# One-core transformer stack on Trainium2: paired decay matmuls, a finer weaving of side chains, and a two-pass layer norm

## The chip, the cores and the metric

The kernel runs on one core of a Trainium2 chip. The metric is the device time of one execution in microseconds. Five engines work side by side and wait for each other by semaphores: TensorE (PE in the profile, its weight loads PEld), VectorE (DVE), ScalarE (ACT), GpSimd (POOL) and SyncE (SP), which here issues the weight transfers. TensorE's clock has two levels, 1.2 and 2.4 GHz; the profile gives the level as the granted clock, 0.50 and 1.00.

## The reference, cut to what matters

One batch of 256 tokens of width 1024 goes through four layers. The first two begin with a mixer of four branches that all read the same projection of the input, and end with a feed-forward part (dense in layer 0, eight experts with two per token in layer 1). The last two are a different block (gated attention, linear attention, cross attention, feed-forward) that the change doesn't touch.

```
y = mixer_block(x, ...)                       # swa, rwkv7, fox, dsa; each gated and projected, then summed
x = layer_norm(4**0.25 * x + y, ln_g, ln_b)   # (x - mu) * rsqrt(var + 1e-5) * g + b
y = swiglu(x) or moe_ffn(x)
x = layer_norm(4**0.25 * x + y, ln_g, ln_b)
```

The branches: swa is window attention with sinks (8 heads), rwkv7 a linear recurrence with a state for each of 4 heads, fox causal attention whose logits get a decay term (the cumulative sum of log-sigmoid gates, query's minus key's, 4 heads), dsa attention over the keys that an index score picks (the 64 best for this mask). All is in float32 to within the kernel's splits.

## The kernel before, in words

**Tiling.** 256 tokens are two tiles of 128 (t = 0, 1). A large product runs on values split in two: each weight chunk that arrives from memory (a `raw` or `af` tile, 128x1024) is copied by ACT to a rounded high part `wh` (line 550) and DVE subtracts to get the low part `wl` (line 552); activations are split the same way (`split`, line 493; `transpose_split`, line 647, transposes four 128x128 blocks on PE and then splits them into `ar` tiles). Three matmuls (high by high, low by high, high by low) then accumulate. The group `mm<-wh,ar` is this work. Everything small (softmax, recurrence, index scores) is in plain float32, which the trace shows as two matmul records for each matmul.

**Weaving in the mixer.** From line 844 on, the mixer lists its weight blocks in a fixed order (`plan`). Inside this part PE's order and the weight transfers on SP are the program's (lines 391, 546). The four branches are Python generators, called chains, that yield at points where PE would have to wait for DVE or ACT. The kernel keeps a counter `vt` of planned PE time (`pe`, line 388; a 128x512 matmul of a chunk counts 512/2.4+13 ns). `yield 6.0` means: not before `vt` has grown by 6.0. After each weight chunk `pump` (line 435) looks whether `vt` grew by `PUMP` since its last turn; if so, each chain that is due issues its next step. A chunk is six 128x512 matmuls, about 1.36 in the counter, or six 128x256 ones, about 0.72. `finish` (line 443) issues what is left of a chain at once, when the main stream needs its result.

**The chains.** `dsa` (line 1022): index scores by PE, then on DVE eight rounds of the eight largest and a replacement, the mask `mk` (line 1053), then `attend`, whose first matmuls add the mask to the logits by an identity matmul (line 809). `fox` (line 982): the cumulative gates give `A` and `B2`; each head's logits are one matmul with 8 rows (line 1014) and one with 64 rows (line 1015). `swa` (line 970) has 64-row logits only. `attend` (line 801) works on two banks of two heads; for heads 0 to 3 it alternates the lower and upper 64 partitions, each half writing to a bank of its own. `_rwkv_tile` (line 1091), once for each token tile: projections, an inverse square root on DVE (line 1147) and a transpose of its result (line 1150), a blocked triangular inverse (lines 1241 to 1265), two chunks of the recurrence (lines 1273 to 1320), a group norm, and the gated result `ofs[t]`. The mixer waits for both rwkv chains at line 947 and transposes their results there (line 948), before branch 1.

**Softmax scaling.** `softmax_pair` (line 764) scales each head's probabilities by the reciprocal sum: in the mixer on ACT (line 785), elsewhere on DVE (line 787).

**Layer norm.** `ln_apply` (line 1382) runs four times: after the mixer and after the feed-forward part of layers 0 and 1, the last without a transpose. For each token tile and each half of 512 columns it makes three passes on DVE (lines 1396 to 1398) and then one `transpose_split` (line 1400).

Of the kernel before, what the change touches and what calls it, by code (L numbers as in the profile page):

```python
# [193 lines left out]
RP = 0  # L194
AHEAD = 0
LOOK = 4
PUMP = 2.0
FIT = 16
AR_SMALL = 512
SMALL = 4  # L200
# [64 lines left out]
class Net:  # L265
# [498 lines left out]
    def softmax_pair(self, lg, nk, scale, sink=None):  # L764

        nm = self.T([128, 2], "nm")
        sm = self.T([128, 2], "sm")
        self.nc.vector.tensor_reduce(nm, lg, axis=AX.X, op=OP.max)  # L768
        if sink is None:
            self.ts(nm, nm, -scale, OP.mult)  # L770
        else:
            self.stt(nm, nm, scale, sink, OP.mult, OP.max)
            self.ts(nm, nm, -1.0, OP.mult)
        P = self.T([128, 2, nk], "P")
        for g in range(2):
            self.act(P[:, g, :nk], lg[:, g, :], AF.Exp, scale=scale, bias=nm[:, g:g + 1], accum_out=sm[:, g:g + 1])
        if sink is not None:
            es = self.T([128, 2], "es")
            self.add(es, sink, nm)
            self.act(es, es, AF.Exp)  # L780
            self.add(sm, sm, es)
        self.nc.vector.reciprocal(sm, sm)
        for g in range(2):
            if self.woven:
                self.act(P[:, g, :nk], P[:, g, :nk], AF.Copy, scale=sm[:, g:g + 1])
            else:
                self.ts(P[:, g, :nk], P[:, g, :nk], sm[:, g:g + 1], OP.mult)
        return P
# [9 lines left out]
        self.act(PT[:, :2 * kt], p)  # L798
        return PT

    def attend(self, t, nk, scale, banks, qk, v, O, f, sinks=(None, None), mask=None, tag="ps"):

        with self.scope():
            kt = nk // 128
            lgs = [self.ps([128, 2, nk]) for _ in banks]
            st = True
            if mask is not None:
                for lg in lgs:
                    self.mmul(lg, self.identb, mask[:, None, :].to_broadcast([128, 2, nk]), True, False)
                st = False  # L810
            for j in range(2):
                for b in range(2):
                    qk(lgs[b][:, j, :], banks[b][j], t, nk, st)
            Ps = [self.softmax_pair(lgs[b], nk, scale, sinks[b]) for b in range(2)]
            yield 6.0
            PTs = []
            for P in Ps:
                PTs.append(self.pT(P, nk, tag))
                self.free(P)
            yield 3.0  # L820
            o = self.bank(tag, [128, 2, 128])
            for j in range(2):
                for k in range(kt):
                    for b in range(2):
                        self.mmul(o[b * 64:(b + 1) * 64, j], v(banks[b][j], k), PTs[b][:, j * kt + k], k == 0, k == kt - 1)
            sl = (slice(None), slice(f, f + 2), slice(t * 128, (t + 1) * 128))
            self.split(O[0][sl], O[1][sl], o)
            yield 1.0


    def mixer(self, l, X, x, st):
# [4 lines left out]
        with self.scope():  # L836
# [55 lines left out]
            O1 = newO(2)  # L892

            rk = self.rwkv(l)
            ofs = {}
            recs = [self.spawn(self.rwkv_tile(l, t, prs, rk, ofs)) for t in range(2)]
            for f, ps in self.lin_fm(X, w, 3):
                self.act(kv[:, 0, :], ps[:, 0])
# [46 lines left out]
            gates(0)  # L945
            for t in range(2):
                self.finish(recs[t])
                self.transpose_split(O1, t, ofs[t])
                self.free(ofs[t])
            branch(1, O1)  # L950
            self.finish(at0)
            self.free(q2)
# [29 lines left out]
    def fox(self, qk_, tv, O):  # L982
        nc = self.nc

        lf = self.T([128, 2, 16], "lf")
        nc.vector.memset(lf, 0.0)
        xx = self.T([128, 2, 4], "fx")
        self.add(xx, tv[:, :, 448:452], self.rrs[:, None, 0:4].to_broadcast([128, 2, 4]))
        e = self.T([128, 2, 4], "fe")
        self.stt(e, xx, -1.0, xx, OP.mult, OP.max)  # L990
        self.act(e, e, AF.Exp, scale=-1.0)
        self.act(e, e, AF.Ln, bias=1.0)
        self.stt(lf[:, :, 0:4], xx, 0.0, e, OP.min, OP.subtract)
        self.ts(lf[:, :, 12:16], lf[:, :, 0:4], -1.0, OP.mult)
        yield 3.0

        p = self.ps([8, 2, 256])
        for g in range(2):
            self.mmul(p[:, g, :], lf[:, 0, g * 8:g * 8 + 8], self.cum0, True, False)
            self.mmul(p[:, g, 128:256], lf[:, 1, g * 8:g * 8 + 8], self.le, False, False)  # L1000
            self.mmul(p[:, g, :], self.sel8[0:1, g, :], self.ones[0:1, :], False, True)
        A = self.T([8, 4, 256], "fA")
        B = self.T([8, 256], "fB")
        for h in range(4):
            self.ts(A[:, h, :], p[:, 0, :], self.hsel[:, h:h + 1], OP.mult)
        self.act(B, p[:, 1, :])
        B2 = self.T([8, 256], "fB2")

        self.ts(B2, B, 8.0, OP.mult)
        yield 3.0  # L1010

        def qk(out, h, t, nk, st):
            sl = slice((h % 2) * 64, (h % 2) * 64 + 64)
            self.mmul(out, A[:, h, t * 128:(t + 1) * 128], B2[:, 0:nk], st, False)
            self.mmul(out, qk_[sl, h // 2, t * 128:(t + 1) * 128], qk_[sl, 2 + h // 2, 0:nk], False, True)

        yield from self.pipeline([
            self.attend(t, 128 * (t + 1), 0.125, ((0, 2), (1, 3)), qk,
                        lambda h, k: tv[:, k, 128 + h * 64:192 + h * 64], O, 0, mask=(self.mc0, self.mc1)[t])
            for t in range(2)])  # L1020

    def dsa(self, q, kd, ki, qi, tv, O):
        nc = self.nc
        REP = -3e38
        for t in range(2):
          with self.scope():
            nk = 128 * (t + 1)
            ww = self.T([128, 4], "ww")
            self.ts(ww, tv[:, t, 452:456], 0.5, OP.mult)
            sc = self.T([128, 256], "sc")  # L1030
            rls = [self.T([128, 2, 256]) for _ in range(2)]
            pk = [self.ps([128, 2, nk]) for _ in range(2)]
            for i in range(2):
                for g in range(2):
                    sl = slice(g * 64, g * 64 + 64)
                    self.mmul(pk[g][:, i], qi[sl, i, t * 128:(t + 1) * 128], ki[sl, 0:nk], True, True)
            for g in range(2):
                self.act(rls[g][:, :, :nk], pk[g], AF.Relu, scale=0.125)
            yield 1.0
            for i in range(2):  # L1040
                for g in range(2):
                    h = 2 * i + g
                    self.stt(sc[:, :nk], rls[g][:, i, :nk], ww[:, h:h + 1], self.ad[:, 256 - nk:] if h == 0 else sc[:, :nk],
                             OP.mult, OP.add)
            self.free(*rls)
            m8 = self.T([128, 8], "m8")
            for r in range(8):
                nc.vector.max(out=m8, in_=sc[:, :nk])
                nc.vector.match_replace(out=sc[:, :nk], in_to_replace=m8, in_values=sc[:, :nk], imm_value=REP)
                if r % 2:  # L1050
                    yield 1.5
            mk = self.T([128, 256], "mk", BF)
            self.ts(mk[:, :nk], sc[:, :nk], -2e38, OP.is_gt, -1e30, OP.mult)

            self.free(sc)

            def qk(out, h, t, nk, st):
                sl = slice((h % 2) * 64, (h % 2) * 64 + 64)
                self.mmul(out, q[sl, h // 2, t * 128:(t + 1) * 128], kd[sl, 0:nk], st, True)

            yield from self.attend(t, nk, 0.125, ((0, 2), (1, 3)), qk, lambda h, k: tv[:, k, 384:448], O, 0, mask=mk[:, :nk])
# [29 lines left out]
    def _rwkv_tile(self, l, t, prs, end, rc, hw, Sts, wa, gu, ofs):  # L1091
# [53 lines left out]
            self.mmul(p[:, 2 * i:2 * i + 2], sq[:, i], self.ind2, True, True)  # L1145
        rs = T([128, 4])
        self.rsqrt(rs, p, [128, 4], 1.0, 1e-12)
        yield 4.0
        p = self.pr([4, 128])
        self.tr(p, rs, self.ident)  # L1150
        rsT = T([4, 128])
# [175 lines left out]
        self.mul(vv, vt.rearrange("p (h s) -> p h s", h=4), bo[:, :, None].to_broadcast([128, 4, 64]))  # L1327
        self.add(o, o, vv)
        self.mul(of, o.rearrange("p h s -> p (h s)"), gm)
        yield 10.0  # L1330

    def groupnorm(self, pY, g, b):
        sm = self.T([128, 4], "gsm")
# [48 lines left out]
    def ln_apply(self, x, l, i, st, X=None):  # L1382

        nc = self.nc
        with self.scope():
# [4 lines left out]
            for t in range(2):  # L1390
                nc.vector.bn_aggr(out=mv[t], in_=st[t])
                self.rsqrt(rs[t], mv[t][:, 1:2], [128, 1], 1.0, 1e-5)
                for b in range(2):
                    sl = slice(b * 512, (b + 1) * 512)
                    v = x[t][:, sl]
                    self.ts(v, v, mv[t][:, 0:1], OP.subtract, rs[t], OP.mult)
                    self.mul(v, v, g[:, sl])
                    self.add(v, v, be[:, sl])
                    if X is not None:
                        last = self.transpose_split(X, t, v, k0=4 * b)  # L1400
                if X is not None and t == HOLD_T:
                    self.hold = (last, 2)
        self.free(*st)
# [731 lines left out]
```

## Time and profile before

| what | value |
|---|---|
| median of 3 runs | 2149.79 us (2149.65 to 2153.29) |
| the profiled execution's own time | 2148.88 us |
| its span, first to last instruction | 2147.2 us |
| PE busy | 2079.5 us (97%) |
| DVE busy | 1495.5 us (70%) |
| ACT busy | 1163.1 us (54%) |
| mean granted clock | 0.981 |
| moved by DMA | 411.37 MB, mean 192 GB/s |

The span is 1.68 us shorter than that execution's time, and that execution 0.91 us below the median. Busy time of PE counts overlapping matmuls once, and a matmul at the lower clock counts as busy as one at the higher. In a timeline row the first two numbers are the start and the length of a run of like instructions; the square bracket at its end is the idle time of the engine just before it and what ended it.

### The profile page before, as it was taken

Reading aid. Unit: us, or ns where it says so; the run is one execution under the profiler, and the core shown is the slowest. Engines: PE = TensorE matmul, PEld = TensorE weight load, DVE = VectorE, ACT = ScalarE, POOL = GpSimd, SP = SyncE. Lnnn points to the kernel's source line nnn. Section 1 sums busy time; section 2 is a strip of 40 time slices with the busy share of each in tenths; the row PEclk is TensorE's granted clock in tenths of the full one; section 3 lists DMA queues with packets and bytes.
Section 4 is the critical chain, followed back from the end, with each engine's and each line's share of the span. In section 5 each row is a group of like instructions: output and inputs, shape, how many; then the busy total and the mean of one; then the engine's idle time right before and its main releaser. Section 6 shows DMA issues by size and latency. Waiting matters only on the chain. (4 is left out here: it accounts for less than half of the span.)

```text
span 2147.2 us, 31339 instructions
## 1 busy us (share of the span) xinstructions
PE 2079.5 (97%) x11520; PEld 1707.0 (80%) x11520; DVE 1495.5 (70%) x2880; ACT 1163.1 (54%) x1756; POOL 42.3 (2%) x111
## 2 busy tenths in 40 slices
PE   8999999998989999999999998999999999999999
PEld 8877777886977777888888887877888777778887
DVE  6774777557676477988888898977645657676453
ACT  5443634443544364677777775575544455555442
POOL 2000000000000000000000000000000000000000
PEclk9998999999999999999999999999999999999999
DMA  7332664552532255599999997536555353554561
GB/s 240 124 114 78 214 204 162 177 196 74 171 129 99 92 176 200 192 348 331 349 327 330 338 316 248 169 129 206 177 191 187 102 171 119 205 180 163 177 196 59
DMA packets 118258, 411.37 MB, mean 192 GB/s; under 512 B 13584, under 2 KB 13745, under 8 KB 118097
## 3 DMA queue, kind: packets, MB, share of 16 engines
q1 hardware_dynamic: 113184, 392.91, 53.2%
q0 software_dynamic: 4912, 16.39, 2.5%
q8 instruction: 92, 1.51, 0.3%
q14 instruction: 70, 0.57, 0.1%
HBM read 408.20 MB, written 1.05 MB: 191 GB/s over the span
## 5 line engine op out<-in xcount | busy, mean ns | idle before, releaser
L382 PE MATMUL mm<-wh,ar 128*128 128x512 f32 (+3 forms) x3200 | 984.8, 389 | 16.2 <-ACT ar L469 7.5
L382 PEld LDWEIGHTS mm<-wh,ar 128*128 128x128 f32 x3200 | 594.2, 191 | 135.0 <-issue 14.6
L482 DVE TENSOR_TENSOR wl<-raw,wh 128x1024 fp32r<-128x1024 f32 (+3 forms) x464 | 547.3, 1191 | 183.3 <-ACT wh L469 174.0
L469 ACT ACTIVATE wh<-raw 128x1024 fp32r<-128x1024 f32 (+3 forms) x464 | 476.1, 1035 | 268.4 <-PE mm L382 155.2
L382 PE MATMUL mm<-wl,ar 128*128 128x512 f32 (+3 forms) x1600 | 617.3, 386 | 0.0
L482 DVE TENSOR_TENSOR wl<-af,wh 128x1024 fp32r<-128x1024 f32 (+2 forms) x300 | 347.0, 1172 | 150.7 <-ACT wh L469 139.1
L469 ACT ACTIVATE wh<-af 128x1024 fp32r<-128x1024 f32 (+2 forms) x300 | 303.7, 1020 | 153.6 <-PE mm L382 55.5
L382 PE MATMUL ps<-wh,ar 128*128 128x512 f32 x1104 | 349.3, 394 | 2.3 <-ACT ar L469 2.3
L382 PEld LDWEIGHTS mm<-wl,ar 128*128 128x128 f32 x1600 | 305.9, 191 | 55.8 <-DVE wl L482 1.0
L382 PEld LDWEIGHTS ps<-wh,ar 128*128 128x128 f32 x1104 | 206.2, 188 | 44.9 <-ACT ar L469 3.9
L382 PE MATMUL ps<-wl,ar 128*128 128x512 f32 x552 | 215.4, 390 | 0.0
L382 PE MATMUL mm<-ar,wh 128*128 128x256 f32 x704 | 133.9, 291 | 0.0
L469 ACT ACTIVATE ar<-pr 128x512 fp32r<-128x512 f32 (+1 forms) x118 | 65.7, 567 | 116.6 <-PE pr L385 101.6
L385 PE MATMUL pr<-ident,af 128*128 128x128 f32 x584 | 96.5, 288 | 30.3 <-DVE af L482 13.8
L382 PEld LDWEIGHTS ps<-wl,ar 128*128 128x128 f32 x552 | 103.7, 188 | 20.8
L385 PEld LDWEIGHTS pr<-ident,af 128*128 128x128 f32 x584 | 68.7, 144 | 60.6 <-issue 25.7
L382 PEld LDWEIGHTS mm<-ar,wh 128*128 128x128 f32 x704 | 111.5, 194 | 3.5 <-issue 2.0
L382 PE MATMUL pr<-wh,ar 128*128 128x512 f32 x352 | 111.6, 395 | 1.2 <-ACT ar L469 1.0
L382 PE MATMUL mm<-ar,wl 128*128 128x256 f32 x352 | 100.5, 285 | 0.0
L482 DVE TENSOR_TENSOR af<-af,af 128x512 f32<-128x512 f32 (+1 forms) x168 | 97.7, 595 | 3.8 <-DMA af<-in_norm_mem_kv_dram 1.6
L469 ACT ACTIVATE af<-af 128x512 f32<-128x512 f32 (+5 forms) x132 | 63.4, 490 | 59.2 <-DVE af L482 40.2
L482 DVE TENSOR_TENSOR ar<-pr,ar 128x512 fp32r<-128x512 f32 (+1 forms) x110 | 70.3, 652 | 32.9 <-ACT ar L469 32.5
(197 smaller groups left out, 1690.5 us busy)
## 6 DMA issues: line engine op xcount, KB each, us to landing
af<-in_e_dram SPq DMA_DIRECT2D x127, 512.0 KB, 5.2
raw<-in_win_dram SPq DMA_DIRECT2D x108, 512.0 KB, 4.5
raw<-in_e_dram SPq DMA_DIRECT2D x81, 512.0 KB, 5.0
af<-in_gu_dram SPq DMA_DIRECT2D x56, 512.0 KB, 4.2
af<-in_w_dram SPq DMA_DIRECT2D x42, 512.0 KB, 4.4
raw<-in_xkv_dram SPq DMA_DIRECT2D x32, 512.0 KB, 4.3
raw<-in_gu_dram SPq DMA_DIRECT2D x32, 512.0 KB, 4.6
af<-in_e_dram SPq DMA_DIRECT2D x38, 384.0 KB, 4.8
```

Source lines behind the costliest of these rows:

```text
L382: return self.pe(self.nc.tensor.matmul(out, lhsT=lhsT, rhs=rhs, start=start, stop=stop, skip_group_check=True), lhsT, rhs)
L385: return self.pe(self.nc.tensor.transpose(out, in_, ident), in_, ident, 1)
L469: return self.nc.scalar.activation(out, in_, f, **kw)
L482: return (eng or self.nc.vector).tensor_tensor(out, a, b, op=op)
```

## The change

- `PUMP` goes from 2.0 to 1.0.
- In the mixer's softmax the first of the two heads is scaled on DVE, the second still on ACT.
- In `fox`, `A` and `B2` are laid out twice, on partitions 0 to 7 and 64 to 71, so that each head's decay matmul reads the partitions on the half of the array on which its query and key lie. `attend` has a parameter `twice`: it goes over the four heads first for the decay matmuls, then for the query-key matmuls.
- `dsa` yields 2.5 before the mask is made and 1.5 after it.
- The yield behind rwkv's inverse square root goes from 4.0 to 6.0, the one at its end from 10.0 to 12.0; the transposes of its result become the chain's own last step, one tile at a time.
- Layer norm makes two passes, `(x - mu) * g` and `* rs + b`, on pieces of 256, 256 and 512 columns, with a transpose behind each.

```diff
-PUMP = 2.0
+PUMP = 1.0
...
         for g in range(2):
-            if self.woven:
+            if self.woven and g:
                 self.act(P[:, g, :nk], P[:, g, :nk], AF.Copy, scale=sm[:, g:g + 1])
...
-            for j in range(2):
-                for b in range(2):
-                    qk(lgs[b][:, j, :], banks[b][j], t, nk, st)
+            for s in ((st, None) if twice else (st,)):
+                for j in range(2):
+                    for b in range(2):
+                        qk(lgs[b][:, j, :], banks[b][j], t, nk, s)
...
-            ofs = {}
+            ofs = {"O": O1}
...
             for t in range(2):
                 self.finish(recs[t])
-                self.transpose_split(O1, t, ofs[t])
-                self.free(ofs[t])
             branch(1, O1)
...
-        A = self.T([8, 4, 256], "fA")
-        B = self.T([8, 256], "fB")
+        A = self.T([72, 2, 256], "fA")
+        B2 = self.T([72, 256], "fB2")
         for h in range(4):
-            self.ts(A[:, h, :], p[:, 0, :], self.hsel[:, h:h + 1], OP.mult)
-        self.act(B, p[:, 1, :])
-        B2 = self.T([8, 256], "fB2")
-        self.ts(B2, B, 8.0, OP.mult)
+            self.ts(A[64 * (h % 2):64 * (h % 2) + 8, h // 2, :], p[:, 0, :], self.hsel[:, h:h + 1], OP.mult)
+        for g in range(2):
+            self.act(B2[64 * g:64 * g + 8], p[:, 1, :], AF.Copy, scale=8.0)
...
-            self.mmul(out, A[:, h, t * 128:(t + 1) * 128], B2[:, 0:nk], st, False)
-            self.mmul(out, qk_[sl, h // 2, t * 128:(t + 1) * 128], qk_[sl, 2 + h // 2, 0:nk], False, True)
+            if st is not None:
+                s8 = slice(sl.start, sl.start + 8)
+                self.mmul(out, A[s8, h // 2, t * 128:(t + 1) * 128], B2[s8, 0:nk], st, False)
+            else:
+                self.mmul(out, qk_[sl, h // 2, t * 128:(t + 1) * 128], qk_[sl, 2 + h // 2, 0:nk], False, True)
...
+            yield 2.5
             mk = self.T([128, 256], "mk", BF)
             self.ts(mk[:, :nk], sc[:, :nk], -2e38, OP.is_gt, -1e30, OP.mult)
             self.free(sc)
+            yield 1.5
...
         self.rsqrt(rs, p, [128, 4], 1.0, 1e-12)
-        yield 4.0
+        yield 6.0
...
         self.mul(of, o.rearrange("p h s -> p (h s)"), gm)
-        yield 10.0
+        yield 12.0
+        self.transpose_split(ofs["O"], t, of)
+        self.free(of)
+        yield 1.0
...
-                for b in range(2):
-                    sl = slice(b * 512, (b + 1) * 512)
+                c = 0
+                for n in (256, 256, 512):
+                    sl = slice(c, c + n)
                     v = x[t][:, sl]
-                    self.ts(v, v, mv[t][:, 0:1], OP.subtract, rs[t], OP.mult)
-                    self.mul(v, v, g[:, sl])
-                    self.add(v, v, be[:, sl])
+                    self.stt(v, v, mv[t][:, 0:1], g[:, sl], OP.subtract, OP.mult)
+                    self.stt(v, v, rs[t], be[:, sl], OP.mult, OP.add)
                     if X is not None:
-                        last = self.transpose_split(X, t, v, k0=4 * b)
+                        last = self.transpose_split(X, t, v, k0=c // 128)
+                    c += n
```

## Rows read from the trace of the kernel before

**Rows 1.** The page: busy time of each engine.

```profile
PE 2079.5 (97%) x11520; PEld 1707.0 (80%) x11520; DVE 1495.5 (70%) x2880; ACT 1163.1 (54%) x1756; POOL 42.3 (2%) x111
```

**Rows 2.** Windows, the two mixers (us; PE, PEld, DVE, ACT, POOL; PEclk; DMA share, GB/s).

```profile
22.00:303.00 281.00, 272.51 (x2044) 220.30 (x2042) 191.69 (x468) 136.61 (x280) 6.58 (x19) 0.96 0.45 153
546.00:833.00 287.00, 274.01 (x2036) 222.11 (x2035) 190.37 (x468) 136.69 (x279) 10.01 (x24) 0.95 0.42 140
```

**Rows 3.** Windows, fox's logits of tile 0 and 1 and what follows each, layer 0.

```profile
163.04:167.60 4.56, 4.56 (x17) 3.16 (x17) 2.12 (x7) 0.38 (x3) 0.07 (x1) 0.67 0.67 225
167.60:171.45 3.85, 3.85 (x23) 2.75 (x22) 1.29 (x5) 1.74 (x6) 0.00 (x0) 0.50 0.01 5
177.93:183.97 6.04, 6.04 (x17) 2.75 (x16) 2.08 (x3) 1.63 (x7) 0.53 (x1) 0.81 0.04 16
183.97:191.96 7.99, 7.99 (x35) 6.08 (x34) 3.14 (x8) 3.41 (x9) 0.00 (x0) 0.50 0.21 68
```

**Rows 4.** Timeline of PE, layer 0: four 64-row logit matmuls in alternate halves (dsa).

```profile
85.19 0.71 PE L382 MATMUL ps<-af,af 64*128 64x128 f32 x8
...
105.58 1.13 PE L382 MATMUL ps<-af,af 64*128 64x256 f32 x8
```

**Rows 5.** Timeline of PE: waits at dsa's masks and at rwkv's transpose, both layers.

```profile
84.89 0.38 PE L382 MATMUL ps<-af,identb 128*128 128x256 bf16 x2 [2.38 <-DVE af L476]
118.16 0.27 PE L385 MATMUL pr<-ident,af 128*4 128x128 f32 x1 [1.90 <-DVE af L482]
124.86 0.59 PE L382 MATMUL ps<-af,identb 128*128 128x512 bf16 x2 [1.14 <-DVE af L476]
...
608.22 0.49 PE L382 MATMUL ps<-af,identb 128*128 128x256 bf16 x2 [2.52 <-DVE af L476]
642.71 0.38 PE L385 MATMUL pr<-ident,af 128*4 128x128 f32 x1 [1.89 <-DVE af L482]
650.37 0.59 PE L382 MATMUL ps<-af,identb 128*128 128x512 bf16 x2 [0.71 <-DVE af L476]
```

**Rows 6.** Windows, PE's work behind four waits, at the lower clock.

```profile
85.84:88.35 2.51, 2.51 (x9) 1.86 (x8) 0.96 (x4) 1.46 (x8) 0.00 (x0) 0.56 0.00 0
608.64:612.19 3.55, 3.55 (x15) 2.80 (x15) 0.96 (x4) 1.34 (x8) 0.00 (x0) 0.56 0.13 51
642.74:645.58 2.84, 2.84 (x14) 2.62 (x14) 2.22 (x10) 1.32 (x2) 0.00 (x0) 0.50 0.86 300
811.03:816.57 5.54, 5.54 (x13) 4.35 (x14) 3.25 (x5) 1.10 (x3) 0.00 (x0) 0.50 0.91 340
```

**Rows 7.** Timeline of PE: branch 1 behind the transposes of rwkv's result, both layers.

```profile
282.07 1.07 PE L382 MATMUL mm<-wh,ar 128*128 128x512 f32 x2 [0.80 <-ACT ar L469]
...
811.03 1.25 PE L382 MATMUL mm<-wh,ar 128*128 128x512 f32 x2 [3.31 <-ACT ar L469]
```

**Rows 8.** Timeline of PE: first transposes after the mixer's and the feed-forward's layer norm, layer 0.

```profile
327.97 0.63 PE L385 MATMUL pr<-ident,af 128*128 128x128 f32 x4 [2.15 <-DVE af L482]
...
532.60 1.94 PE L385 MATMUL pr<-ident,af 128*128 128x128 f32 x8 [5.30 <-DVE af L482]
```

**Rows 9.** Layer-norm passes: timeline of DVE, and a group by line, operation and shape.

```profile
529.65 1.00 DVE L476 TENSOR_SCALAR af<-af,af 128x512 f32<-128x512 f32 x2
530.56 2.49 DVE L482 TENSOR_TENSOR af<-af,af 128x512 f32<-128x512 f32 x4
...
L479 DVE SCALAR_TENSOR_TENSOR af<-mm,af,af 128x512 f32<-128x512 f32 x26 | 19.3, 747 | 37.0 <-PE mm L382 37.0
```

**Rows 10.** Timelines: ACT's copy in the recurrence behind a weight copy; chain runs on PE.

```profile
137.50 1.06 ACT L469 ACTIVATE wh<-raw 128x1024 fp32r<-128x1024 f32 x1
138.58 0.28 ACT L469 ACTIVATE af<-pr 64x128 f32<-64x128 f32 x1
...
147.44 0.44 PE L385 MATMUL pr<-ident,af 128*128 128x128 f32 x2
...
153.40 0.68 PE L382 MATMUL pr<-id,af 64*64 64x64 f32 x16 [0.47 <-ACT af L469]
```

More of the change, by code (lines that the diff above doesn't have):

```diff
@@ L799, in pT, with attend @@
         return PT
-    def attend(self, t, nk, scale, banks, qk, v, O, f, sinks=(None, None), mask=None, tag="ps"):
+    def attend(self, t, nk, scale, banks, qk, v, O, f, sinks=(None, None), mask=None, tag="ps", twice=False):
         with self.scope():
@@ L1013, in qk @@
             sl = slice((h % 2) * 64, (h % 2) * 64 + 64)
-            self.mmul(out, A[:, h, t * 128:(t + 1) * 128], B2[:, 0:nk], st, False)
-            self.mmul(out, qk_[sl, h // 2, t * 128:(t + 1) * 128], qk_[sl, 2 + h // 2, 0:nk], False, True)
+            if st is not None:
[3 more added lines that the diff above has]
+                self.mmul(out, qk_[sl, h // 2, t * 128:(t + 1) * 128], qk_[sl, 2 + h // 2, 0:nk], False, True)
         yield from self.pipeline([
             self.attend(t, 128 * (t + 1), 0.125, ((0, 2), (1, 3)), qk,
-                        lambda h, k: tv[:, k, 128 + h * 64:192 + h * 64], O, 0, mask=(self.mc0, self.mc1)[t])
+                        lambda h, k: tv[:, k, 128 + h * 64:192 + h * 64], O, 0, mask=(self.mc0, self.mc1)[t], twice=True)
             for t in range(2)])
```

## The prediction

> **What bounds the kernel now.** I read the page first: PE is busy 97% of the span, DVE 70%, ACT 54% [rows 1]. So PE sets the time, and what can be won lies in three places: PE's idle time, work on PE that could overlap, and stretches at the lower clock, which count as busy. The windows view of the two mixers (columns: the stretch, its length, the busy time and count of PE, PEld, DVE, ACT, POOL, the granted clock, the DMA share and GB/s) shows all three [rows 2]: of 281 and 287 us PE idles 8.5 and 13 us, and the mean clock is 0.96 and 0.95, below 1, while DVE is busy two thirds and ACT half. DVE and ACT have room; PE's order there is fixed, so every wait of a chain holds up all work behind it. I then read PE's timeline for the waits and the windows for the clock.
>
> **Fox's logits.** Today 8-row and 64-row matmuls alternate, and nothing overlaps. Tile 0 takes 4.56 us for eight matmuls, tile 1 6.04 [rows 3], partly at clock 0.67 and 0.81 on average. Four 64-row matmuls in alternate halves take 0.71 us at the narrow size and 1.13 at the wide one [rows 4]: two run side by side. After the change there are two such groups of four, one with 8 rows and one with 64. If the 8-row group pairs as well, a tile costs 2 x 0.71 = 1.42 and 2 x 1.13 = 2.26, and a layer saves 3.14 + 3.78 = 6.9. No row shows two 8-row matmuls in different halves; if they don't overlap, each costs at most today's mean, 4.56/8 = 0.57 and 6.04/8 = 0.76, and a layer saves 3.5. I take 6.9, since the halves and banks are the same as in the pairs of [rows 4], times two layers (the second repeats the pattern): **13.8**, low end 7. Making A and B2 stays four DVE and two ACT operations, DVE has one less; it lies in the chain and I count nothing.
>
> The Trainium skill says in TensorEngine Tiling (Key Properties) that changing the tiling mode drains TensorE, while tiles of one mode run independently. By that rule today's alternation pays a drain each time and grouping alone would win part of it, so the low end would be nearer 10 than 7; the forecast is the same.
>
> **The clock behind fox.** PE is busy throughout both stretches, yet behind each the clock is 0.50: for 3.85 us and 7.99 us [rows 3]. It falls inside fox's groups and comes back once wide matmuls have run. If the shorter, paired groups leave it up, half of 11.84 us, 5.9, is the most a layer can win, and nothing the least. I take 5, as small matmuls don't quite double at the lower clock, and take the clock as kept, because the groups become a third as long and then look like the paired logits of [rows 4]. Two layers: **10**.
>
> **More room in dsa.** PE waits at the masks for DVE's selection: 2.38, 1.14, 2.52 and 0.71 us [rows 5], in all 6.75. The added 4.0 of planned time (2.5 before the mask, 1.5 behind) is about three chunks, more than the longest wait. The cover is weight matmuls that exist anyway; the chain ends later, but dsa has tens of us until branch 3 needs it. With the cover gone (the main stream out of chunks) the waits would come back. **6.75**, low end 0.
>
> **rwkv's inverse square root.** Two waits of 1.90 and 1.89 [rows 5], **3.8**; the yield grows by 2.0, one or two chunks, just enough. Behind three of these six waits PE works at 0.50 to 0.56 [rows 6], 8.9 us together in its first three rows, so at most 4.4 more; I take **3.4**. Against both I set 2.8 for waits that remain, since DVE's queue is what is late there and the change doesn't shorten it.
>
> **rwkv's result.** Its transposes stand right before branch 1; PE then waits 0.80 and 3.31 us for ACT's split, which sits behind weight copies [rows 7]. As a step of the chain they run earlier: eight transposes, four ACT and four DVE operations for both layers, no DMA moved, on queues with room [rows 2]. The wait should go (**4.1**), and the 5.54 us at 0.50 behind the longer one [rows 6] gives up to 2.8; I take **2.3**. A step of its own costs switching PE there and back, an estimate of 0.15 each, 0.6 in all. What is late next is DVE's gate product.
>
> **Layer norm.** A first pass now costs 0.46 a half: two run 1.00 with their overlap, and the next starts 0.91 behind the first; the other passes 0.60, from four in 2.49 [rows 9]. The new pass has two tensors and a per-partition scalar; its nearest row runs 0.75 [rows 9], some 0.66 from start to start. A half falls from 1.66 to 1.32, but two pieces of 256 cost perhaps 1.6, so DVE gains only 0.4 a tile, less a third split. More comes from order: the first transpose needs two short passes, not three long ones behind the other half's. PE's waits there are 2.15 and 5.30 [rows 8]. I take 1.5 at each of these two, 0.5 at each of the other two norms: **4**, ends 0 and 8.
>
> **Softmax scaling** goes from ACT to DVE for 16 heads a layer, some 0.3 us each. It is hidden under the chunks between `attend`'s steps; without that cover 5 us a layer at most. I count nothing.
>
> **The finer pump.** It moves no work, but a due chain is advanced one chunk sooner, so its step can find DVE or ACT behind: ACT's small copy in the recurrence starts only behind a weight copy of 1.06 us [rows 10]. I count about 84 rwkv steps with yields up to 1.5. In the stretch from 147.44 to 153.40, where five chain runs already stand one chunk or less apart, one waits, 0.47 [rows 10]: 0.09 a step on average, **8** lost; ends 0 and 39 (0.47 at each).
>
> **Sum.** 13.8 + 10 + 6.75 + 3.8 + 3.4 + 4.1 + 2.3 + 4 = 48.1 us won, 8 + 0.6 + 2.8 = 11.4 given back, net 36.7. The profiled execution took 2148.88, so 2112.2; it lies 0.91 below the median of the runs shown, so **2113**.
>
> **Rivals.**
> *The clock falls in fox all the same.* For it: these groups stay narrow, and it fell today without any idle time. Then the 10 go, and some 3 of the groups' own saving: 2126. The Trainium skill, in TensorE: Matmul & The Clock Gate (Part 1), has the gate follow how busy PE has been; by that rule a PE that is busy all through gives no reason for the fall, and pairing none for its absence. The trace disagrees in so far as PE has no idle time in [rows 3]. Chance 0.13.
> *The room doesn't help.* DVE has queued more by then, and dsa's and rwkv's waits stay: 6.75 + 3.8 + 3.4 less the 2.8 already set aside, 11 lost: 2124. Against it: DVE is idle a third of the stage [rows 2]. Chance 0.12.
> *The finer pump does nothing*, because yields of 1.5 still need two wide chunks of 1.36: the 8 aren't lost, 2105. Chance 0.08.
> *Slower:* the recurrence outruns DVE and ACT. If each of the 84 steps has to wait behind a weight copy or a low part for 0.7 us, 59 us are lost instead of 8: 2164. It turns slower than before from about 0.53 us a step. Against it: four of the five close runs above don't wait. Chance 0.07.
>
> **How the numbers follow.** The forecast has 0.58, the rivals 0.40; 0.02 stay for no change. The forecast's own ends (layer norm 0 to 8, pump 0 to 16, fox's pairing) give some 10 either way; the low end reaches past the idle pump to 2098, the high end past both middle rivals, nearly to where both hold together: 2136. What a measurement of this kernel can tell from no change is about 0.2%, 4.3 us. Every case but the slower one is over that: faster 0.89, same 0.03, slower 0.08.
>
> **What would show it.** Right: fox's groups near 1.4 and 2.3 us with clock 1.00 behind them; no wait over 0.5 at the masks and at the 4-column transpose; no wait in front of branch 1; mixers some 16 us shorter each; norms' waits 1 to 2 us shorter. Wrong: many new waits under 1 us at the small 64-row matmuls, a clock of 0.50 behind fox, 8-row matmuls that start one after the other, or a mixer with DVE near full.

## The result and the profile after

The changed kernel takes **2116.51 us** (median of 4 runs, 2113.92 to 2118.59); the kernel before took 2149.72 beside it (2146.31 to 2153.29). The ratio is 0.9845, 95% interval 0.9825 to 0.9865: 33 us faster. The forecast was 2113, range 2098 to 2136. The profiled execution took 2118.59, its span is 2116.9.

The page's busy line, after, against [rows 1]:

```profile
PE 2051.8 (97%) x11520; PEld 1688.7 (80%) x11520; DVE 1495.5 (71%) x2916; ACT 1153.3 (54%) x1732; POOL 41.4 (2%) x111
```

The span fell by 30.3 us and PE's busy time by 27.7. So nearly all of the gain is work on PE that got shorter, not waits that went: PE's idle time over the span is 65.1 us where it was 67.7.

The two mixers in the windows view (columns as in [rows 2]; from the first 128x256 weight matmuls to the first output projection, behind which the windows of [rows 2] run on for 1.5 and 0.6 us):

```profile
21.26:284.90 263.64, 256.71 (x2039) 211.06 (x2037) 189.85 (x481) 131.25 (x264) 6.97 (x19) 1.00 0.48 162
531.67:800.32 268.65, 259.47 (x2040) 213.05 (x2038) 192.22 (x484) 131.28 (x264) 8.98 (x23) 0.99 0.47 150
```

The clock is 1.00 and 0.99 where [rows 2] had 0.96 and 0.95. In the traces' clock records the stretches at 0.50 that begin in the mixers last 51.2 us together before and 6.8 after; 34.1 of the 51.2 begin inside fox's groups. An estimate from these: as the lower level is half the upper, the 44.4 us less are worth at most 22 of what the mixers win. Fox's logits and what follows them, tile 0 and tile 1, against [rows 3]:

```profile
159.37:160.66 1.29, 1.29 (x18) 1.05 (x17) 0.98 (x5) 0.70 (x1) 0.00 (x0) 1.00 0.45 121
160.66:165.77 5.11, 5.11 (x36) 3.76 (x34) 4.94 (x23) 3.52 (x10) 0.00 (x0) 1.00 0.48 176
169.28:171.41 2.13, 2.13 (x18) 1.38 (x17) 2.13 (x3) 0.61 (x3) 0.00 (x0) 1.00 0.15 62
171.41:180.28 8.87, 8.87 (x97) 7.34 (x95) 6.67 (x17) 4.33 (x13) 0.00 (x0) 1.00 0.45 144
```

The groups take 1.29 and 2.13 us instead of 4.56 and 6.04, and the stretches behind them run at 1.00 instead of 0.50. PE's waits, in its timeline: rwkv's inverse square root, which [rows 5] had one step earlier; the mask of window attention in mixer 1; the end of each mixer, for [rows 7]; the layer norms of layer 0, for [rows 8]:

```profile
113.75 0.71 PE L382 MATMUL pr<-af,E 4*128 4x128 f32 x4 [0.60 <-DVE af L482]
...
267.79 0.73 PE L382 MATMUL mm<-wh,ar 128*128 128x512 f32 x2 [1.60 <-DVE af L482]
...
746.00 0.39 PE L382 MATMUL ps<-ms,identb 128*128 128x512 bf16 x1 [1.89 <-DVE ar L482]
...
781.94 0.73 PE L382 MATMUL mm<-wh,ar 128*128 128x512 f32 x2 [2.30 <-DVE af L482]
...
311.32 0.81 PE L385 MATMUL pr<-ident,af 128*128 128x128 f32 x4 [2.03 <-DVE af L479]
...
321.86 1.05 PE L385 MATMUL pr<-ident,af 128*128 128x128 f32 x4 [1.94 <-DVE af L479]
...
507.73 0.80 PE L385 MATMUL pr<-ident,af 128*128 128x128 f32 x4 [2.04 <-DVE af L479]
509.07 0.66 PE L385 MATMUL pr<-ident,af 128*128 128x128 f32 x4 [0.54 <-DVE ar L482]
517.64 1.09 PE L385 MATMUL pr<-ident,af 128*128 128x128 f32 x4 [7.92 <-DVE af L479]
```

All four of dsa's mask waits are gone. ACT's wait in front of branch 1 is gone, but a wait for DVE has come at the same end of the mixer, and another at window attention's mask, 1.79 us in mixer 0 and 1.89 in mixer 1, where the kernel before has none. PE's idle time in the mixers, 8.5 and 13.0 us by [rows 2], is 6.9 and 9.2: 5.4 us less. The norm ahead of the second mixer waits longer than before: 7.92 where one of 5.30 was the longest.

This table is worked out from the starts of the matmuls in PE's timeline: *mixer*, from its first long run of weight matmuls to the first output projection; *norms*, from there to the second mixer's first; *rest*, from the second output projection to the last matmul. The other kernels are some of those of the experiments.

| us | mixer 0 | norms, feed-forward | mixer 1 | rest |
|---|---|---|---|---|
| before | 291.7 | 232.7 | 298.2 | 1310.3 |
| after | 275.2 | 235.1 | 280.3 | 1312.5 |
| before, fox alone | 281.9 | 232.6 | 280.6 | 1312.7 |
| before, finer pump alone | 295.0 | 233.1 | 296.9 | 1311.6 |
| after, old pump | 291.4 | 235.0 | 280.4 | 1309.1 |
| after, no room | 281.6 | 234.9 | 281.9 | 1309.9 |
| after, old norm | 274.9 | 234.4 | 280.7 | 1312.3 |
| after, hold to tile 1 in both layers | 276.4 | 228.3 | 278.7 | 1319.1 |
| after, hold to tile 1 in layer 0 | 275.4 | 228.4 | 276.7 | 1312.4 |

The mixers win 34.4 us, the norms' stretch loses 2.4, the rest 2.2.

### The profile page after: what moved, and what is told of

Its sections match the earlier page's. It is cut to its first block, busy times and chain, and to the rows that moved or that the text cites. A ratio compares the mean times of both kernels' runs of the same rounds, so it can differ in the third digit from the quotient of the medians.

```text
span 2116.9 us, 31337 instructions
## 1 busy us (share of the span) xinstructions
PE 2051.8 (97%) x11520; PEld 1688.7 (80%) x11520; DVE 1495.5 (71%) x2916; ACT 1153.3 (54%) x1732; POOL 41.4 (2%) x111
## 5 line engine op out<-in xcount | busy, mean ns | idle before, releaser
L382 PEld LDWEIGHTS mm<-wh,ar 128*128 128x128 f32 x3200 | 588.3, 190 | 128.7 <-issue 14.2
L382 PE MATMUL pr<-af,af 64*64 64x32 f32 (+8 forms) x1132 | 84.4, 244 | 2.3 <-ACT af L469 2.3
```

Of the source, the lines that this page charges most:

```text
L382: return self.pe(self.nc.tensor.matmul(out, lhsT=lhsT, rhs=rhs, start=start, stop=stop, skip_group_check=True), lhsT, rhs)
```

## The experiments

The kernel before took from 2145.1 to 2149.4 us (medians) beside these runs, so ratios to it are compared, and a ratio is turned into microseconds on 2149.7; the intervals are 95%.

### Fox: order or halves?

Two kernels, each undoing one of the two things that the new logits do. In one, grouped but with all 8-row operands in one half:

```diff
-        A = self.T([72, 2, 256], "fA")
+        A = self.T([8, 4, 256], "fA")
...
-                self.mmul(out, A[s8, h // 2, t * 128:(t + 1) * 128], B2[s8, 0:nk], st, False)
+                self.mmul(out, A[:, h, t * 128:(t + 1) * 128], B2[:, 0:nk], st, False)
```

> The changed kernel with fox's 8-row matmuls grouped ahead of the 64-row ones as now, but with A and 8*B all on partitions 0 to 7, so that no two 8-row matmuls lie in different halves. Theory H (the overlap of the halves is what shortens the 8-row group): the group costs about twice as much, 1.4 and 2.3 us instead of 0.6 and 1.1, some 2 us a layer; with it the clock falls again behind the groups in each layer, 5 us a layer: about 2130 in all. Theory S (the switch between 8-row and 64-row matmuls was the price, and grouping takes it away): the 8-row group stays under 1.1 and 1.6 us, the clock stays up: 2118.

In the other, both halves, but head by head as before:

```diff
-            if st is not None:
-                s8 = slice(sl.start, sl.start + 8)
-                self.mmul(out, A[s8, h // 2, t * 128:(t + 1) * 128], B2[s8, 0:nk], st, False)
-            else:
-                self.mmul(out, qk_[sl, h // 2, t * 128:(t + 1) * 128], qk_[sl, 2 + h // 2, 0:nk], False, True)
+            s8 = slice(sl.start, sl.start + 8)
+            self.mmul(out, A[s8, h // 2, t * 128:(t + 1) * 128], B2[s8, 0:nk], st, False)
+            self.mmul(out, qk_[sl, h // 2, t * 128:(t + 1) * 128], qk_[sl, 2 + h // 2, 0:nk], False, True)
...
-                        ..., mask=(self.mc0, self.mc1)[t], twice=True)
+                        ..., mask=(self.mc0, self.mc1)[t])
```

> The changed kernel with A and 8*B in both halves, but the 8-row and the 64-row matmul of a head one behind the other again, as in the kernel before. Theory H (it is the overlap of the halves): pairs of heads lie in different halves, so most of the gain stays; the groups take 1.5 to 2 us and 2.3 to 3 us, the clock stays up, 2117 to 2119. Theory S (each switch between 8 and 64 rows is paid): the groups take as long as before, 4.5 and 6 us, and the clock falls behind them: 7 + 5 us a layer, about 2140.

Measured: one half 0.9865 (0.9839 to 0.9891), 4 us slower than the changed kernel, intervals overlapping; alternating 0.9918 (0.9894 to 0.9943), **16 us slower**. PE's timeline of the kernel with one half (start, duration):

```profile
159.24 1.15 PE L382 MATMUL ps<-af,af 8*128 8x128 f32 x8
160.32 0.71 PE L382 MATMUL ps<-af 64*128 64x128 f32 x8
...
169.60 1.99 PE L382 MATMUL ps<-af,af 8*128 8x256 f32 x8
171.52 1.13 PE L382 MATMUL ps<-af 64*128 64x256 f32 x8
```

of the changed kernel, with both halves:

```profile
159.37 0.71 PE L382 MATMUL ps<-af,af 8*128 8x128 f32 x8
160.01 0.72 PE L382 MATMUL ps<-af 64*128 64x128 f32 x8
```

and of the alternating one:

```profile
159.87 0.48 PE L382 MATMUL ps<-af,af 8*128 8x128 f32 x2
160.28 0.48 PE L382 MATMUL ps<-af 64*128 64x128 f32 x2
160.70 0.48 PE L382 MATMUL ps<-af,af 8*128 8x128 f32 x2
```

From start to start, four 8-row matmuls in one half take 1.08 us, 0.27 each, and over two halves 0.64, 0.16 each, while alternating ones follow each other at 0.41 to 0.42, although neighbouring heads lie in different halves. The step to the next head, which writes another bank, costs the same as the step within a head, so it isn't the shared bank. In the kernel before, with all 8-row operands in one half, the step is 0.41 too until the clock falls, and some 0.72 from there: with alternation the second half gains nothing. So it is the order that pays: in layer 0, alternating takes 3.3 + 5.6 us (the window below stops 0.39 us short of the second group's end), grouping 1.76 + 3.00, and the second half takes off a further 0.5 and 0.9. The windows of the alternating kernel show the clock fall again, as in [rows 3], with PE busy throughout:

```profile
159.87:163.20 3.33, 3.33 (x18) 2.36 (x17) 2.43 (x11) 0.72 (x2) 0.00 (x0) 1.00 0.58 177
163.95:167.30 3.35, 3.35 (x22) 2.37 (x22) 1.31 (x8) 1.39 (x3) 0.00 (x0) 0.50 0.16 64
173.33:178.50 5.17, 5.17 (x17) 2.54 (x16) 2.89 (x3) 0.61 (x3) 0.00 (x0) 0.91 0.34 112
177.61:187.85 10.24, 10.24 (x44) 7.01 (x44) 4.26 (x13) 4.55 (x13) 0.00 (x0) 0.50 0.00 0
```

With one half it stayed at 1.00 behind both groups, behind the second by this window:

```profile
172.60:181.50 8.90, 8.90 (x98) 7.36 (x96) 6.89 (x17) 4.33 (x13) 0.00 (x0) 1.00 0.30 94
```

Theory S holds for the time and the clock. For the 8-row group alone the truth lies between the two: 1.08 and 1.92 us in one half, where S had under 1.1 and 1.6 and H 1.4 and 2.3. What H has right is worth 1.3 us a layer. The profile of the alternating kernel is of its slowest execution (2138.36, median 2132.61), so it shows the effect at its largest.

The Trainium skill's rule in TensorEngine Tiling (Key Properties), that a change of tiling mode drains TensorE, would give the alternating order its longer steps; the 0.41 against 0.27 agrees, but no run shows that 8-row and 64-row matmuls are different modes.

**Fox's new logits alone, in the kernel before** (the edit is the diff's part in `fox` and `attend`).

> The kernel before with fox's new logits alone (8-row matmuls grouped and in both halves), all else as before. The forecast's terms: 13.8 for the groups and 10 for the clock behind them, 23.8 won: 2149.7 - 23.8 = 2126. Theory Q (the clock is only in part fox's doing): the alternating order in the changed kernel cost 16.1, the 8-row group in one half 3.3 of it or beside it, so 16 to 17 won: 2133. Rival, the other waits of the kernel before take a part of it back (PE reaches dsa's and rwkv's waits sooner): 10 won, 2140.

Measured 0.9873 (0.9852 to 0.9895): **27 us** of the 33. The two mixers lose 27.5 us in the table, though PE waits only 2.8 us less in them. The forecast's size, 23.8, holds within the interval; the rival that other waits take it back falls. Against this kernel the changed one is only 6 us faster (0.9845 to 0.9873, intervals overlapping): that is what the five other parts win together.

### The pump and the room

Threshold 2.0 again in the changed kernel:

```diff
-PUMP = 1.0
+PUMP = 2.0
```

> The changed kernel with the old pump threshold of 2.0 instead of 1.0. The forecast's term (a chain run one chunk sooner finds DVE or ACT behind, 8 us lost over 84 steps): 2108.5, the waits of 0.3 to 0.5 us at the small 64-row matmuls gone. Rival N (yields of 1.5 need two chunks either way, the pump does nothing): 2116. Rival L (the finer pump is what lets the chains end in time): new or longer waits at the ends of the two mixers, where recurrence, dsa and window attention are finished, 4 us or more, 2121 and over.

The added yields taken out again:

```diff
-            yield 2.5
...
-            yield 1.5
...
-        yield 6.0
+        yield 4.0
```

> The changed kernel without the added yields in dsa (2.5 and 1.5) and at the inverse square root (6.0 back to 4.0). Forecast's terms: dsa's mask waits 6.75, the rwkv transposes' 3.8 and 3.4 of clock behind them come back, less the 2.8 set aside: 11 us slower, 2127.5. Rival (with the other changes the selection is done in time anyway): under 3 us, 2117 to 2119. Under a finer pump the waits could also be longer than before, since each chain step comes a chunk sooner: up to 2133.

The finer pump alone in the kernel before:

```diff
-PUMP = 2.0
+PUMP = 1.0
```

> The kernel before with the pump threshold of 1.0 instead of 2.0, all else as before. The forecast's term: chain steps come a chunk sooner and find DVE or ACT behind, 8 us lost: 2158. Theory E (the finer pump by itself brings the chains forward, and the main order no longer runs out of chunks ahead of a chain's end): 12 to 22 us won, as its undoing cost in the changed kernel: 2128 to 2138. Theory I (it pays only together with the longer yields, since a coarse pump rounds each of them up): within 4 us of the kernel before, 2146 to 2154.

Measured: old pump 0.9966 (0.9952 to 0.9979), **26 us slower** than the changed kernel; no room 0.9899 (0.9881 to 0.9917), 12 slower; finer pump alone 1.0004 (0.9991 to 1.0018), no change. So the finer pump alone wins nothing, and in the changed kernel taking out either of the two loses. The longer yields alone in the kernel before were not run; the nearest is the changed kernel with the old pump, 20 us slower than fox alone. The timelines show why. The finer pump without room: PE is at dsa's masks too early (first the finer pump alone, then the changed kernel without room):

```profile
81.80 0.38 PE L382 MATMUL ps<-af,identb 128*128 128x256 bf16 x2 [3.71 <-DVE af L476]
...
612.54 0.58 PE L382 MATMUL ps<-af,identb 128*128 128x256 bf16 x2 [5.85 <-DVE af L476]
```

```profile
82.56 0.58 PE L382 MATMUL ps<-af,identb 128*128 128x256 bf16 x2 [3.71 <-DVE af L476]
...
598.64 0.59 PE L382 MATMUL ps<-af,identb 128*128 128x256 bf16 x2 [3.08 <-DVE af L476]
```

where [rows 5] had 2.38 and 2.52. Room without the finer pump: everything comes late. The mask of tile 1 in layer 0 stands at 144.23 us where the kernels before and after have it at 124.86 and 124.57, and fox's first cumulative sum at 177.92 instead of 154.01 and 152.37, with a wait of its own:

```profile
121.15 1.22 PE L382 MATMUL pr<-af,E 4*128 4x128 f32 x4 [3.15 <-DVE af L482]
...
177.92 1.02 PE L382 MATMUL ps<-cum,af 128*8 128x256 f32 x2 [4.83 <-DVE af L479]
```

Around these the clock is down, in the windows of the same kernel:

```profile
119.36:129.60 10.24, 8.45 (x56) 6.37 (x56) 8.00 (x24) 2.33 (x3) 0.00 (x0) 0.67 0.33 103
177.40:187.60 10.20, 9.68 (x45) 5.68 (x46) 2.52 (x7) 1.00 (x4) 0.00 (x0) 0.50 0.46 130
```

Without room, the two marks stand at 118.41 and 141.79, and with the finer pump alone at 119.31 and 142.69: the finer pump brings the chain some 6 us forward at the mask and 12 at fox, the room puts it back, and in the changed kernel they cancel. That the coarse pump delays it because it rounds each longer yield up to whole pairs of chunks is argued from the program; that it is late is shown. In this profile mixer 1 was spared (280.4), and this execution was the fastest of twelve (2131.31, median 2138.62).

**Pump at 0.5** (`-PUMP = 1.0`, `+PUMP = 0.5`), on the kernel with the hold moved in layer 0 (below, ratio 0.9828).

> The kernel that beat both so far with the pump threshold at 0.5 instead of 1.0, so that chains are also advanced behind chunks shorter than 1.0 of planned time. Theory E (the sooner a due step is issued, the better): 2103 to 2107. Saturation (most chunks are over 1.0 already): 2107 to 2110. The forecast's mechanism (steps too close behind each other find DVE and ACT behind): 2112 and over, with more waits of 0.3 to 1 us at the small 64-row matmuls.

Measured 0.9819 (0.9798 to 0.9839): no difference in the sum. But it isn't saturated, as things do move: fox's logits of tile 0 start at 154.32 us instead of 160.20, mixer 0 takes 272.2 us where that kernel has 275.4, and mixer 1 takes 282.5 instead of 276.7, with a wait of 4.49 for DVE at one of the recurrence's 64-row matmuls (a slower execution, 2115.17, median 2110.93).

### The recurrence's result

The transposes back in the main order, in front of branch 1; the chain's last yield goes back to 10.0 with them.

```diff
                 self.finish(recs[t])
+                self.transpose_split(O1, t, ofs[t])
```

> The changed kernel with the rwkv result's transposes back in front of branch 1 in the main order instead of in the chain. Forecast's terms: PE waits there for ACT's split again, 4.1 us in both layers, with 2.3 of clock, less 0.6 for the switches: 5.8 slower, 2122. Rival (the wait was only handed on: PE now waits 1.60 and 2.30 at the end of the mixers for DVE's gate product, and these go when the other comes back): 2 us or less, 2116 to 2118.5.

Measured 0.9884 (0.9866 to 0.9902): 8 us slower. ACT's waits are back:

```profile
270.66 0.96 PE L382 MATMUL mm<-wh,ar 128*128 128x512 f32 x2 [2.32 <-ACT ar L469]
...
788.31 0.96 PE L382 MATMUL mm<-wh,ar 128*128 128x512 f32 x2 [2.40 <-ACT ar L469]
```

4.72 us, against 1.60 + 2.30 for DVE at this place in the changed kernel. So the wait was handed on nearly whole, as the rival said, yet the time moved as the forecast said. But what PE waits for there in the changed kernel is no gate product. In DVE's timeline,

```profile
777.79 3.50 DVE L482 TENSOR_TENSOR wl<-raw,wh 128x1024 fp32r<-128x1024 f32 x3 [1.65 <-ACT wh L469]
781.21 0.68 DVE L482 TENSOR_TENSOR af<-mm,af 128x512 f32<-128x512 f32 x1
```

the wait ends with the second row, by the program the sum of branch 0's gate with its bias (`add(g, ps, gb)` in `gates`), which stands behind the low parts of three weights.

Both mixers are longer (281.5 and 283.3) with hardly more idle time, but the stretches at a clock of 0.50 that begin in them last 20.5 us together, where the changed kernel has 6.8. This is the slowest of its four executions (2126.34, median 2120.93). Why the clock falls more there stays open.

### The layer norm

The old three passes in the changed kernel:

```diff
-                for n in (256, 256, 512):
...
-                    self.stt(v, v, mv[t][:, 0:1], g[:, sl], OP.subtract, OP.mult)
-                    self.stt(v, v, rs[t], be[:, sl], OP.mult, OP.add)
+                    self.ts(v, v, mv[t][:, 0:1], OP.subtract, rs[t], OP.mult)
+                    self.mul(v, v, g[:, sl])
+                    self.add(v, v, be[:, sl])
```

> The changed kernel with the old layer norm (three passes over halves of 512 instead of two passes over pieces of 256, 256 and 512). Theory O, order on DVE: with the short pieces the last split of tile 0 ends sooner, the held low parts of four weights are let go sooner, and they land between the tiny steps of tile 1's inverse square root. With the old passes the hold is let go later, only about one low part comes between, and PE's waits at the norm ahead of the second mixer fall from 2.04 + 0.54 + 7.92 to about 2.2 + 2.1 + 5.3; the norm behind the first mixer loses its new wait of 1.94: 4 us faster than the 2116.5 of the changed kernel, 2112.5. Theory P, the norm's own price is the forecast's (the new passes win 4 and something else in the stretch lost 8): 2120.5.

Measured 0.9844 (0.9821 to 0.9866): **no difference**. Its waits ahead of the second mixer are those of the kernel before, 9.56 us in all, where the last three rows of the changed kernel's waits make 10.50 (here the old passes; below, the kernel before, which [rows 8] follows with 5.30):

```profile
508.20 0.63 PE L385 MATMUL pr<-ident,af 128*128 128x128 f32 x4 [2.15 <-DVE af L482]
510.93 1.09 PE L385 MATMUL pr<-ident,af 128*128 128x128 f32 x4 [2.10 <-DVE af L476]
517.32 1.94 PE L385 MATMUL pr<-ident,af 128*128 128x128 f32 x8 [5.31 <-DVE af L482]
```

```profile
523.58 0.63 PE L385 MATMUL pr<-ident,af 128*128 128x128 f32 x4 [2.15 <-DVE af L482]
526.31 0.98 PE L385 MATMUL pr<-ident,af 128*128 128x128 f32 x4 [2.10 <-DVE af L476]
```

What DVE does in the 7.92 us is in the changed kernel's timeline of DVE:

```profile
511.86 0.21 DVE L479 SCALAR_TENSOR_TENSOR af<-af 128x1 f32<-128x1 f32 x1
511.99 1.10 DVE L482 TENSOR_TENSOR wl<-raw,wh 128x912 fp32r<-128x912 f32 x1
513.01 0.15 DVE L479 SCALAR_TENSOR_TENSOR af<-af 128x1 f32<-128x1 f32 x1
513.08 1.10 DVE L482 TENSOR_TENSOR wl<-raw,wh 128x912 fp32r<-128x912 f32 x1
514.10 0.22 DVE L479 SCALAR_TENSOR_TENSOR af<-af 128x1 f32<-128x1 f32 x1
514.23 1.22 DVE L482 TENSOR_TENSOR wl<-raw,wh 128x1024 fp32r<-128x1024 f32 x1
515.36 0.15 DVE L479 SCALAR_TENSOR_TENSOR af<-af 128x1 f32<-128x1 f32 x1
515.43 1.22 DVE L482 TENSOR_TENSOR wl<-raw,wh 128x1024 fp32r<-128x1024 f32 x1
```

Each tiny step of tile 1's inverse square root has a weight's low part of 1.1 to 1.2 us behind it, four in all. The program holds low parts back until tile 0's last split (`self.hold`); with shorter pieces that split ends earlier in tile 1's sequence. So the hold was moved to tile 1, first for both layers:

```diff
-                if X is not None and t == HOLD_T:
+                if X is not None and t == 1:
```

> The changed kernel, but the layer norms that feed a matmul let the held low parts of weights go behind tile 1's last split instead of tile 0's. Theory O (the low parts between tile 1's inverse square root steps cost the time): the wait of 7.92 falls by the four low parts of 1.1 to 1.2 us, to about 3.3, the wait of 1.94 at the other norm goes, some 6 us in all: 2110. Rival, the low parts are wanted at once: PE then waits for them at the first weight matmuls behind the norm, four times 1.2 us later, and the time stays at 2116 or goes up to 2121. Theory P (passes or third split are the cost): no change at the transposes, 2116.

Measured 0.9837 (0.9816 to 0.9858), no difference in the sum, but the table shows both theories at work: 6.8 us won in layer 0's stretch, 6.6 lost behind the second mixer. There a weight's low part comes too late, and the clock falls (windows 832 to 838: 0.58):

```profile
832.27 0.80 PE L382 MATMUL mm<-wl,ar 128*128 128x512 f32 x1 [2.43 <-DVE wl L482]
```

Then for layer 0 alone:

```diff
-                if X is not None and t == HOLD_T:
+                if X is not None and t == (1 if l == 0 else 0):
```

> The changed kernel with the held low parts let go behind tile 1's last split, now only for the two norms of layer 0; layer 1's norm lets them go behind tile 0's, as in the changed kernel. Theory O (order on DVE, each norm by what it feeds): layer 0's stretch from its output projection to the second mixer's first matmul keeps the 6.9 us that it won with both norms changed (235.1 to 228.3), and the loss of 6.6 behind the second mixer, with a wait of 2.43 for a weight's low part and a low clock behind it, is gone: 2109. Rival, the loss behind the second mixer comes from the whole later order and not from that norm's hold: it stays, 2115.

Measured **0.9828** (0.9813 to 0.9844), median 2108.53. DVE's timeline now has tile 1's steps in one piece, and PE's wait is half:

```profile
509.21 1.30 DVE L479 SCALAR_TENSOR_TENSOR af<-af 128x1 f32<-128x1 f32 x6
510.55 1.55 DVE L479 SCALAR_TENSOR_TENSOR af<-af,af,af 128x256 f32<-128x256 f32 x3
```

```profile
511.19 1.09 PE L385 MATMUL pr<-ident,af 128*128 128x128 f32 x4 [3.96 <-DVE af L479]
```

By the ratio this is 4 us better than the changed kernel, with intervals that overlap; what carries it is the stretch itself, 228.3 to 229.9 us in the four kernels with this hold in layer 0, against 233.3 to 235.1 in the changed kernel and its six variants without it. No version found beats this one by more than the intervals.

### Softmax scaling

On that kernel, the first head's scaling back on ACT:

```diff
-            if self.woven and g:
+            if self.woven:
```

> The kernel that beat both so far (low parts held to tile 1's end for layer 0's norms) with the softmax scaling of the first head of each pair back on ACT. The forecast counted nothing for this part: 2108.5, plus or minus 2. Theory V (DVE's queue is what ends most of PE's remaining waits, so 0.3 us less on it for 16 heads a layer shows): 3 us or more faster, 2105 and under. Theory A (ACT's queue is the later one in attention): 3 us or more slower, 2112 and over.

Measured 0.9823 (0.9803 to 0.9844): nothing, as counted.

## Why the prediction was right, and where it was not

**The whole.** 2116.5 against 2113: PE's fixed order bounds the kernel, and the gain lies in the mixers, 34.4 us where the forecast's mixer terms net 32.7. That it comes so near is partly luck: the terms have 14.65 us of waits go and 2.8 of them stay, and PE's idle time in the mixers fell by 5.4 only, as new waits came elsewhere; the 8 charged to the pump cover about that gap. Without fox the forecast's parts net 12.9, and 6 were measured.

**Fox's logits, 13.8.** Right: 7.2 us in layer 0 by [rows 3] and the rows after, 7.0 in layer 1. The 8-row matmuls do overlap in two halves. But the larger part, 5.8 of the 7.2, is there with grouping in one half, which the text counted only in its low bound, at 3.5. Part of it is clock: up to the fall tile 0's steps take 0.41 us, and 0.72 from there. For A and B2, DVE has four operations instead of five, but ACT two instead of one.

**The clock behind fox, 10.** Right in size: fox alone won 27; less 14.2 for the groups and 2.8 for waits that got shorter, some 10 are left, with the uncertainty of the 27. The reason given, that paired and shorter groups look like dsa's, is half right: pairing isn't needed, as grouped but unpaired groups of 1.76 and 3.00 us kept the clock as well, while alternating ones of 3.3 and 5.6 did not. Every alternating group is also longer than every sorted one, so whether the order or the length decides is not shown. The clock rival is out.

**Room, 6.75 + 3.8 + 3.4 - 2.8 = 11.2.** The mask and transpose waits are gone, and undoing it costs 12. But this is no measure of what it wins over the kernel before: it was measured only beside the finer pump, and what it adds is part of the 6 that pump, room, transposes, norm and softmax win together.

**The finer pump, 8 lost.** Wrong as a price of its own. Alone it costs 1 us, 4 at most: PE's waits in the mixers do grow, by 6.3 us, nearly half of it at dsa's masks (9.56 against 6.75), where the forecast put all of it on the recurrence, and PE's other time in the mixers falls by 4.3. Beside the longer yields its undoing costs 26. The step that failed is treating pump and yields as two terms that add: they set the same thing, where a chain stands against the main order. At the small matmuls, where the forecast had its price, little came: 7 waits of 0.3 us or more at matmuls with 64 rows, 3.1 us in all, against 5 and 2.6 before. The new waits stand at window attention's mask, 1.79 and 1.89 us; with the old pump they are absent, but with a threshold of 0.5 too, so that they are the pump's price is not shown. The rival that it does nothing holds for the pump alone and not beside the room; the one that ends slower is out.

**The recurrence's result, 4.1 + 2.3 - 0.6.** The size held (8 when undone), the wait did not go: 3.9 us stand there for another operation of DVE. The text named DVE as what is late next, with the wrong operation and no price: it is a gate's bias sum behind three low parts. The 0.6 for the switches is an estimate for which the text names no row; in the traces of the kernels before and after, the second weight matmul behind a group of 128-row transposes starts 0.31 us after the first instead of 0.23, so 0.09 a step instead of 0.15.

**Layer norm, 4 won.** Wrong: nothing was won; its stretch got 2.4 us longer, and with the old passes in the changed kernel it is hardly shorter (234.4), so most of the 2.4 isn't the new passes' doing. The failed step is "more comes from order": it counted the passes and not the low parts that tile 0's last split lets go. Moving these won 6.7 us in that stretch.

**What doesn't add up.** Fox alone, and room, transposes and norm each undone, make 27 + 12 + 8 + 0 = 47 us; with the pump's forecast price it would be 39, and 33 were measured, 6 beside fox. The parts overlap: what undoing one costs in the changed kernel isn't what adding it wins. Each of these has an uncertainty of 4 to 5 us.

## What to carry to other kernels

Sort small matmuls by their row count before pairing them in halves: here switching cost more than lying in one half, and the lower clock behind it came on top (some 10 us beside 14.2). A scheduler's step and its yields are one setting: change them together, and look at where a chain's marks stand. Before shortening a chain on an engine, see which held work its end lets go.

## What was not expected

The clock fell at fox although PE had no idle time there in the kernel before or in the undoing, and the same matmuls in another order kept it. It fell in or right behind all 12 groups of the three kernels that alternate (before, finer pump alone, and the undoing), and in none of the 44 groups of the eleven kernels that sort, paired or not, nor in the 10 us behind them.

The Trainium skill, in TensorE: Matmul & The Clock Gate (Part 1), ties the gate to how busy PE has been; the 3.35 and 10.24 us at 0.50 above, with PE busy, as the profile counts it, for all of both stretches and of the groups before, are not told by that.

The times of one kernel's runs go along with their mean granted clock: the twelve with the old pump reach from 2131.31 us at 0.986 to 2144.59 at 0.979. By an estimate from these, 0.7% of 2138 us is 15, and the difference is 13.
